# A Conformer convolution whose last channels, layer norm and second product run in two token halves, with weights parted ahead

## The chip, the cores and the metric

The kernel runs on one core of one Trainium2 chip. Its time is device microseconds (us) of one execution. Engines are named as in the profile: PE is TensorE (matmuls; PEld its weight loads), DVE is VectorE, ACT is ScalarE, POOL is GpSimd, SP is SyncE, which here only issues transfers.

## The reference

Two layers over 512 tokens of 1024 channels. Each is a half-step feed-forward, a token mixer and another half-step feed-forward; the mixer of layer 0 is the convolution module that the change is about, that of layer 1 is an attention.

```python
def swiglu_ffn(x, w_gate, w_up, w_down):          # D 1024, F 2816
    return (jax.nn.silu(x @ w_gate) * (x @ w_up)) @ w_down

def conformer_conv(x, w_pw1, b_pw1, w_dw, b_dw, ln_g, ln_b, w_pw2, b_pw2):
    h = x @ w_pw1 + b_pw1                          # 1024 -> 2048
    a, gate = jnp.split(h, 2, axis=-1)
    h = a * jax.nn.sigmoid(gate)
    h = lax.conv_general_dilated(h, w_dw, ...) + b_dw   # causal, 31 taps, each channel by itself
    h = jax.nn.silu(layer_norm(h, ln_g, ln_b))     # mean and variance over the 1024 channels of a token
    return h @ w_pw2 + b_pw2                       # 1024 -> 1024

# layer 0:
h = h + 0.5 * swiglu_ffn(rms_norm(h, ffn1_norm[0]), ...)
h = h + conformer_conv(rms_norm(h, mix_norm[0]), ...)
h = h + 0.5 * swiglu_ffn(rms_norm(h, ffn2_norm[0]), ...)
```

## The kernel before

Activations lie with channels on the 128 partitions and the 512 tokens along the free axis, so a tensor of 1024 channels is eight chunks of 128x512. All is in float32; a product is made of three matmuls on parts: each operand is parted into a rounded high part and the remainder, and `mm3` multiplies high x high, high x low and low x high into one PSUM bank (lines 186 to 188). Weights come from DRAM in units of 128x1024 (512 KB). `fetch` loads a unit on SP's queue into `raw`, ACT casts it to `whi`, and the remainder `wlo` is a subtraction (lines 127 and 128) on DVE, or on POOL for the units 68 to 83 (`POOL_UNITS`), which are the sixteen of the first pointwise product. Three buffers of each are used, and `unit()` takes the oldest pair and starts the next fetch. `weight_order` lists the units in the order of use.

A feed-forward (`ffn`) goes in thirds of its hidden chunks: for each chunk two products `pg` over eight channels of input, Silu and multiplication, parting into `hhi` and `hlo`; then eight products `pd` of the third. The first feed-forward has 44 + 24 units. The convolution stage follows, from the first `pa` product (372.4 us of the profiled execution) to the first `pg` of the next feed-forward (606.6). It does this, per chunk of channels `ch`:

- `gated(ch)`: two products `pa` (48 matmuls), scaled on DVE by the norm's factor `rb`, sigmoid on ACT, the gated product `gl` (with 30 zero columns ahead of the tokens), which is parted into `glh` and `gll` (POOL).
- the 31 taps, each a shifted copy of `gl` times one weight per channel, are dealt out to three engines. `PE_TAPS[ch]` of them are matmuls by diagonal matrices (`taps_pe`, tile `pc`; the diagonals are made on ACT, the first 30 of them during the first feed-forward); `POOL_TAPS[ch]` are scaled on ACT (`pr`) and added on POOL into `accp`, one of the tiles `ws` (line 439); the rest are fused multiply-adds on DVE into `pc` (line 450). Then DVE makes `y` of the parts (line 452).
- statistics: POOL adds `y` into `dsum` and its square into `dsq` (ACT squares).

All of it is at the full 512 tokens. Then comes the layer norm: `token_sums` are matmuls of one column that give the sums over channels, 128 tokens to a column (tiles `ms` and `mq`); DVE takes the variance and its inverse root on tiles of 4 columns (`inv_root`, lines 222 to 230), `spread` brings the mean (`pb_lm`) and the root (`pb_lr`) back to 128x512 with diagonals on ACT and two matmuls, and DVE and POOL subtract the mean. Each chunk is then multiplied by the root, goes through Silu and is parted into `shi` and `slo`. Only then can the second pointwise product start (`second`, tiles `pp`): three outputs together, then five one by one, 192 matmuls of 512 columns. Its results are added to the residual `res`, which lies in the tile `xpar`, and go into the next norm (`n_f2.chunk`).

The order of the instructions on each engine is set by a scheduler when the program is built (it simulates the program as it is written), with a few `tc.issue_after` as bounds. An engine works through its own list strictly in order.

## Time and profile before

| | |
|---|---|
| time, median of three runs | 1993.03 us (1990.7, 1993.03, 1993.52) |
| the profiled execution's own time | 1991.78 us |
| its span in the profile | 1990.1 us |
| mean granted clock of TensorE | 0.981 of full speed |
| busy: PE | 1916.1 us, 96% of the span |
| busy: PEld (weight loads, beside PE) | 1582.6 us, 80% |
| busy: DVE | 1105.6 us, 56% |
| busy: ACT | 751.0 us, 38% |
| busy: POOL | 207.2 us, 10% |
| DRAM traffic | 89 GB/s over the span |

The span is what the profiler recorded of one execution, and the time is somewhat longer than it. Busy time of PE contains overlaps, since matmuls are pipelined: one of 512 columns is shown with 389 ns where the next starts about 0.23 us after it. "Granted clock" is the share of full speed that the chip gave TensorE in a stretch. A row "A <- B" in the table of waits says how long the first engine's instruction waited in sum, and which instruction of which engine released it.

### The profile page before, as it was taken

The page shows a single profiled execution, that of the slowest core. Times are in us where ns is not written, and L with a number is a line of the kernel's source. Part 1 is how long each engine was busy: PE and PEld are TensorE (multiplying, and loading weights), DVE is VectorE, ACT ScalarE, POOL GpSimd, SP SyncE. Part 2 cuts the span into 40 slices and gives each one's busy share as a digit, 9 for nine tenths or more (in the row PEclk, how much of TensorE's full clock was granted, in tenths as well). Part 3 has the DMA queues.
Part 4 walks back from the last instruction along what each step waited for, and adds up shares of the span by engine and source line. Part 5 has one row for each costly group of instructions (what it writes and reads, how often), then busy time and mean ns, then how long its engine had stood idle before and what let it go on. Part 6 is the DMA issues. An engine that isn't in the chain of part 4 may idle for free.

```text
span 1990.1 us, 22242 instructions
## 1 busy us (share of the span) xinstructions
PE 1916.1 (96%) x8705; PEld 1582.6 (80%) x8705; DVE 1105.6 (56%) x1604; ACT 751.0 (38%) x1135; POOL 207.2 (10%) x186
## 2 busy tenths in 40 slices
PE   9999999997579999999999999999999899999997
PEld 6888888886468888888888888887888688888885
DVE  6434434779865434434754444466999754444344
ACT  8323222544553322222432222345777733222222
POOL 0000000374600000000000000002554100000000
PEclk9999999999689999999999999999999999999998
DMA  5333332322013333332333233243223133333321
GB/s 164 98 102 96 96 96 80 111 64 74 1 53 96 96 96 95 97 95 79 112 106 96 95 96 96 90 138 112 72 75 104 48 96 95 96 96 96 98 90 66
DMA packets 54361, 181.98 MB, mean 91 GB/s; under 512 B 6256, under 2 KB 6384, under 8 KB 54256
## 3 DMA queue, kind: packets, MB, share of 16 engines
q1 hardware_dynamic: 53680, 179.52, 29.3%
q8 instruction: 68, 1.11, 0.2%
q10 hardware_dynamic: 576, 1.05, 0.1%
q14 instruction: 37, 0.30, 0.0%
HBM read 172.15 MB, written 4.19 MB: 89 GB/s over the span
## 4 chain that ended last, share of the span: by engine, by line
PE 93%; DVE 5%; ACT 1%; issue 1%; POOL 0%; DMA 0%; SPq 0%; DVEq 0%; ACTq 0%; POOLq 0%
PE pg L186 16%; PE pg L188 16%; PE pg L187 16%; PE pd L187 8%; PE pd L186 8%; PE pd L188 8%; DVE pc L450 3%; PE z L666 2%; PE pa L187 1%; PE pa L188 1%; PE pa L186 1%; PE po L186 1%; PE pv L186 1%; PE pq L186 1%; PE pq L187 1%; PE pv L188 1%
## 5 line engine op out<-in xcount | busy, mean ns | idle before, releaser
L127 ACT CAST whi<-raw 128x1024 fp32r<-128x1024 f32 (+2 forms) x329 | 338.4, 1030 | 1020.3 <-PE pg L187 344.9
L186 PE MATMUL pg<-xhi_f,whi 128*128 128x512 f32 x1408 | 548.3, 390 | 2.8 <-ACT xhi_f L248 1.5
L187 PE MATMUL pg<-xlo_f,whi 128*128 128x512 f32 x1408 | 548.0, 389 | 1.6 <-DVE xlo_f L249 1.6
L188 PE MATMUL pg<-xhi_f,wlo 128*128 128x512 f32 x1408 | 547.7, 389 | 0.1
L128 DVE TENSOR_TENSOR wlo<-raw,whi 128x1024 fp32r<-128x1024 f32 (+2 forms) x313 | 377.5, 1207 | 68.1 <-ACT whi L127 67.7
L186 PEld LDWEIGHTS pg<-xhi_f,whi 128*128 128x128 f32 x1408 | 264.3, 188 | 60.6 <-ACT xhi_f L248 2.8
L187 PEld LDWEIGHTS pg<-xlo_f,whi 128*128 128x128 f32 x1408 | 264.3, 188 | 57.7 <-DVE xlo_f L249 3.0
L188 PEld LDWEIGHTS pg<-xhi_f,wlo 128*128 128x128 f32 x1408 | 264.3, 188 | 55.3 <-DVE wlo L128 0.5
L187 PE MATMUL pd<-hlo,whi 128*128 128x512 f32 x704 | 273.2, 389 | 0.0
L186 PE MATMUL pd<-hhi,whi 128*128 128x512 f32 x704 | 272.6, 389 | 0.0
L188 PE MATMUL pd<-hhi,wlo 128*128 128x512 f32 x704 | 272.6, 389 | 0.0
L304 DVE TENSOR_TENSOR tu<-pg,r_f 128x512 f32<-128x512 f32 x88 | 60.8, 691 | 260.2 <-PE pg L188 259.9
L317 DVE SCALAR_TENSOR_TENSOR xpar<-pd,xpar 128x512 f32<-128x512 f32 x96 | 66.0, 691 | 244.4 <-PE pd L188 244.4
L302 DVE TENSOR_TENSOR tg<-pg,r_f 128x512 f32<-128x512 f32 x88 | 60.8, 691 | 173.7 <-PE pg L188 173.3
L186 PEld LDWEIGHTS pd<-hhi,whi 128*128 128x128 f32 x704 | 132.1, 188 | 27.5
L188 PEld LDWEIGHTS pd<-hhi,wlo 128*128 128x128 f32 x704 | 132.1, 188 | 27.5
L187 PEld LDWEIGHTS pd<-hlo,whi 128*128 128x128 f32 x704 | 132.1, 188 | 27.3
L450 DVE SCALAR_TENSOR_TENSOR pc<-gl,xpar,pc 128x512 f32<-128x512 f32 x141 | 97.5, 746 | 8.6 <-PE pc L188 4.4
L127 ACT CAST hhi<-tu 128x512 fp32r<-128x512 f32 x88 | 55.0, 625 | 68.2 <-DVE tu L305 68.2
L128 POOL TENSOR_TENSOR wlo<-raw,whi 128x1024 fp32r<-128x1024 f32 x16 | 38.7, 2417 | 400.2 <-ACT whi L127 400.2
L565 POOL TENSOR_SCALAR_AFFINE_SELECT tri<-ones 128x128 f32<-128x128 f32 x1 | 0.3, 295 | 734.7 <-DVE tu L305 734.7
L128 DVE TENSOR_TENSOR hlo<-tu,hhi 128x512 fp32r<-128x512 f32 x88 | 60.4, 686 | 8.9 <-ACT hhi L127 8.9
(248 smaller groups left out, 2295.4 us busy)
## 6 DMA issues: line engine op xcount, KB each, us to landing
raw<-in_gu_dram SPq DMA_DIRECT2D x175, 512.0 KB, 3.5
raw<-in_dna_dram SPq DMA_DIRECT2D x64, 512.0 KB, 3.5
raw<-in_dnb_dram SPq DMA_DIRECT2D x32, 384.0 KB, 3.1
raw<-in_pw_dram SPq DMA_DIRECT2D x24, 512.0 KB, 3.5
raw<-in_kq_dram SPq DMA_DIRECT2D x16, 512.0 KB, 3.8
raw<-in_wv_dram SPq DMA_DIRECT2D x8, 512.0 KB, 3.6
raw<-in_wo_dram SPq DMA_DIRECT2D x8, 512.0 KB, 4.2
away<-xpar SPq DMA_DIRECT2D x8, 256.0 KB, 2.1
```

The lines of the kernel that those rows point to most:

```text
L127: ins = A.copy(dst_hi, src)
L128: (G if on_pool else V).tensor_sub(dst_lo, src, dst_hi.bitcast(F32))
L186: PE.matmul(ps, w[0], x[0], start=first, stop=False)
L187: PE.matmul(ps, w[0], x[1], start=False, stop=False)
L188: PE.matmul(ps, w[1], x[0], start=False, stop=last)
L302: V.tensor_mul(tg, pt[0], rb)
L304: V.tensor_mul(tu, pt[1], rb)
L317: V.scalar_tensor_tensor(res[d], pd, 0.5, res[d], op0=ALU.mult, op1=ALU.add)
L450: V.scalar_tensor_tensor(acc, x, q, acc, op0=ALU.mult, op1=ALU.add)
L565: G.affine_select(out=tri, in_=ones, compare_op=ALU.is_ge, fill=0.0, base=0, pattern=[[-1, P]], channel_multiplier=1,)
L666: PE.matmul(dst, st, m[:, a:b], start=False, stop=True, skip_group_check=True)
```

## The change

The change touches the convolution stage, and the first feed-forward ahead of it.

1. **Weights parted ahead.** The 24 units of the two pointwise products are loaded during the first feed-forward, one after each hidden chunk from the third on and two in each row of `pd` products (`part_ahead`). ACT casts them, POOL makes the remainder, and both parts are stored to DRAM (`aparth`, `apartl`), 48 stores issued on ACT's queue. In the convolution `fetch` loads the two parts (2 x 512 KB) straight into `whi` and `wlo`; no cast and no remainder is left there.
2. **Token halves.** Channels 5, 6 and 7 (`HALVED`) go through their taps, statistics and `y` in two halves of 256 tokens. The layer norm and the second product are made once for each half. For the second half the outputs come in the order 5, 6, 7, 0, 1, 2, 3, 4 (`SECOND`); the weights of 5, 6 and 7 are still there, those of the other five are loaded a second time.
3. **Other tables.** `PE_TAPS` and `POOL_TAPS` have new entries, with rows of their own for the second halves; 8 diagonals instead of 30 are made ahead and 30 instead of 6 buffers hold the others; `accp` goes through three tiles instead of two.
4. **A planned order.** `Plan` collects every step of the stage with its engine, an estimated duration, what it reads and writes, a rank and the buffers it takes. `issue` goes through them like a list scheduler (the step that can start first, then by rank) and writes the instructions in that order, under `tc.manual_schedule` for PE, DVE, ACT and POOL.
5. Small: the next feed-forward sums over channels in the order in which they became ready (`norm.order`); the pool `x2` opens after the first feed-forward.

The core of the diff:

```diff
-PE_TAPS = [5, 5, 5, 5, 6, 6, 9, 14]
-POOL_TAPS = [5, 5, 5, 5, 5, 5, 5, 4]
-POOL_UNITS = range(68, 84)
-AHEAD = 30
-E_BUFS = 6
+PE_TAPS = [0, 3, 3, 4, 6, 9, 9, 9]
+POOL_TAPS = [10, 10, 10, 10, 10, 9, 9, 9]
+PE_TAPS_2 = [0, 0, 0, 0, 0, 14, 14, 14]
+POOL_TAPS_2 = [0, 0, 0, 0, 0, 8, 8, 8]
+HALVED = 5
+TOKENS = (slice(0, T // 2), slice(T // 2, T))
+SECOND = (5, 6, 7, 0, 1, 2, 3, 4)
+AHEAD = 8
+E_BUFS = 30
+class Plan:
+    LATE = 0.15
+    SELF = {"V": 0.14, "A": 0.1, "G": 0.02}
+    def add(self, engine, work, do, r=(), w=(), rank=0):
+        ...
+    def issue(self):
+        ...
+                key = (t, steps[n][4])
+                if best is None or key < best[0]:
+                    best = (key, n, new)
...
         yield from feed_forward(0)
-        for c in range(NC):
-            yield pw1[c, 0]
-            yield pw1[c, 1]
-        for d in range(NC):
-            yield pw2[d]
+        for i in range(2 * NC):
+            yield apart[i]
+        for d in (*range(NC), *SECOND[3:]):
+            yield apart[2 * NC + d]
...
+    def part_ahead(p):
+        if behind:
+            i, pair = behind.pop()
+            away = []
+            for n, x in zip("hl", pair):
+                d = spill.tile([P, UNIT], F32, name=f"apart{n}{i}")
+                nc.scalar.dma_start(d, x.bitcast(F32))
+                away.append(d)
+            apart.append(tuple(away))
+        if parting:
+            src, i = parting.pop(0), len(apart)
+            raw = p.tile([P, UNIT], F32, name=f"praw{i}", tag="praw", bufs=2)
+            hi = p.tile([P, UNIT], F32R, name=f"phi{i}", tag="phi", bufs=2)
+            lo = p.tile([P, UNIT], F32R, name=f"plo{i}", tag="plo", bufs=2)
+            nc.sync.dma_start(raw, src)
+            split(hi, lo, raw, on_pool=True)
+            behind.append((i, (hi, lo)))
...
+        if isinstance(src, tuple):
+            pair = []
+            for j, n in enumerate(("whi", "wlo")):
+                t = wp.tile([P, UNIT], F32R, name=f"{n}{i}", tag=n, bufs=3)
+                nc.sync.dma_start(t.bitcast(F32), src[j])
+                pair.append(t)
+            ready.append(tuple(pair))
+            return
...
-            split(hi[:, sl], lo[:, sl], raw[:, sl], on_pool=i in POOL_UNITS)
+            split(hi[:, sl], lo[:, sl], raw[:, sl])
...
+                    if beside is not None and (third or f > 1):
+                        with tc.issue_after(last[0].ins):
+                            beside(pp_)
...
+                    if beside is not None and d in (2, 5):
+                        with tc.issue_after(last[0].ins):
+                            beside(pp_)
...
-    ffn(0, n_f1, n_mix.chunk, early=early_diagonals)
+    parting += [pw1[c, o] for c in range(NC) for o in range(2)] + [pw2[d] for d in range(NC)]
+    ffn(0, n_f1, n_mix.chunk, early=early_diagonals, beside=part_ahead)
...
+        def layer_norm(h, rank):
+            sl, n = TOKENS[h], T // 2
...
+            add("PE", 1.0, lambda: token_sums(ms(), dsum[:, sl], y[NC - 1]()[:, sl]), r=[f"dsum{h}", y7], w=[ms], rank=rank)
...
+                if ch % 2 == 0:
+                    add("V", 0.36, lambda yc=yc: V.tensor_sub(yc(), yc(), lm()), r=[lm], w=[yt], rank=rank)
+                else:
+                    add("G", 0.74, lambda yc=yc: G.tensor_sub(yc(), yc(), lms), r=["lms"], w=[yt], rank=rank)
...
+            gate(ch)
...
+            diagonals(ch, 2 * ch + 1, PE_TAPS[ch])
+            depthwise(ch, TOKENS[0] if ch >= HALVED else ALL, 2 * ch + 3)
+        layer_norm(0, 40)
+        second(0, (0, 1), 50, True)
+        for d in range(2, NC):
+            second(0, (d,), 50 + d, True)
+        for ch in range(HALVED, NC):
+            diagonals(ch, 42, PE_TAPS_2[ch])
+            depthwise(ch, TOKENS[1], 42)
+        layer_norm(1, 45)
+        second(1, SECOND[:2], 90, False)
+        second(1, SECOND[2:3], 91, False)
+        with tc.manual_schedule(engines={nc.tensor.engine, nc.vector.engine, nc.scalar.engine, nc.gpsimd.engine}):
+            plan.issue()
+        for d in SECOND[:3]:
+            n_f2.chunk(d)
+        for d in SECOND[3:]:
+            w = unit()
+            pp = ps.tile([P, T], F32, name=f"pp{d}_1", tag="bank", bufs=8)[:, : T // 2]
...
-        second((0, 1, 2))
-        for d in range(3, NC):
-            second((d,))
```

What stands in a row on an engine shows what the planner made of it. A row is line, operation, result<-operands and the size of the tile; the number behind a name tells its buffer.

On PE, between the last product of the taps and the second pointwise product, before (`pc7` is the last chunk's taps, `ms` and `mq` the sums, `pb_` the spread rows, `pp` the second product):

```order
L426 MATMUL pc7_3806<-y0h_2773,mshift_2726 128x512
L217 MATMUL ms_3937<-onesD_75,dsum_2771 128x1 x4
L217 MATMUL ms_3937<-onesD_75,y7_3930 128x1 x4
L217 MATMUL mq_3964<-onesD_75,dsq_2772 128x1 x4
L217 MATMUL mq_3964<-onesD_75,sqy7_3933 128x1 x4
L207 MATMUL pb_lm_3950<-dg_lm_0_3951,onesr_73 128x512
L207 MATMUL pb_lm_3950<-dg_lm_1_3957,onesr_73 128x512
L207 MATMUL pb_lr_3991<-dg_lr_0_3992,onesr_73 128x512
L207 MATMUL pb_lr_3991<-dg_lr_1_3998,onesr_73 128x512
L186 MATMUL pp0_4078<-shi0_4014,whi84_3554 128x512
L186 MATMUL pp1_4079<-shi0_4014,whi85_3699 128x512
```

And in the changed kernel (`pc7_256` is the second token half of the last chunk, `pb_lm0` and `pb_lr0` belong to the first half's layer norm, `pp0_0` is output 0 of the first half):

```order
L325 MATMUL pc7_256_4257<-glh7_4024,d229_4220 128x256
L326 MATMUL pc7_256_4257<-gll7_4039,d229_4220 128x256
L327 MATMUL pc7_256_4257<-glh7_4024,d229_4220 128x256
L728 MATMUL pb_lm0_4372<-dg_lm0_0_4339,onesr_73 128x256
L325 MATMUL pc7_256_4257<-glh7_4024,d230_4239 128x256
L326 MATMUL pc7_256_4257<-gll7_4039,d230_4239 128x256
L327 MATMUL pc7_256_4257<-glh7_4024,d230_4239 128x256
L728 MATMUL pb_lm0_4372<-dg_lm0_1_4359,onesr_73 128x256
L669 MATMUL pc7_256_4257<-y0h_2886,mshift_2876 128x256
L728 MATMUL pb_lr0_4406<-dg_lr0_0_4396,onesr_73 128x256
L728 MATMUL pb_lr0_4406<-dg_lr0_1_4399,onesr_73 128x256
L325 MATMUL pp0_0_4436<-shi0_4419,whi84_3767 128x256
```

Nothing stood between the sums and `pp0` but the spread rows; now the taps of the other half stand among them, to the end of `pc7_256`.

On DVE, the layer norm's small steps, before:

```order
L450 SCALAR_TENSOR_TENSOR acc7_3916<-gl7_3763,xpar_70,acc7_3916 128x512
L454 TENSOR_TENSOR y7_3930<-acc7_3916,y7_3930 128x512
L488 COPY sm_3936<-ms_3937 128x4
L196 CAST dp_lm_3947<-sm_3936 128x4
L494 TENSOR_TENSOR sm_3936<-sm_3936 128x4
L197 TENSOR_TENSOR dp_lm_3947<-sm_3936,dp_lm_3947 128x4
L495 TENSOR_TENSOR sm_3936<-mq_3964,sm_3936 128x4
L496 TENSOR_SCALAR sm_3936<-sm_3936 128x4
L223 TENSOR_SCALAR sm_3936<-sm_3936 128x4
L224 TENSOR_SCALAR sm_3936<-sm_3936 128x4
```

And now, in the first half's layer norm (`sm0` has two columns for each quantity):

```order
L690 SCALAR_TENSOR_TENSOR pc6_256_4166<-gl6_3758,xpar_70,pc6_256_4166 128x256 x3
L713 COPY sm0_2889<-ms0_4309 128x2
L690 SCALAR_TENSOR_TENSOR pc6_256_4166<-gl6_3758,xpar_70,pc6_256_4166 128x256
L719 CAST dp_lm0_2890<-sm0_2889 128x2
L720 TENSOR_TENSOR dp_lm0_2890<-sm0_2889,dp_lm0_2890 128x2
L690 SCALAR_TENSOR_TENSOR pc6_256_4166<-gl6_3758,xpar_70,pc6_256_4166 128x256
L737 TENSOR_TENSOR sm0_2889<-sm0_2889 128x2
L738 TENSOR_TENSOR sm0_2889<-mq0_4322,sm0_2889 128x2
L739 TENSOR_SCALAR sm0_2889<-sm0_2889 128x2
L363 TENSOR_SCALAR sm0_2889<-sm0_2889 128x2
L364 TENSOR_SCALAR sm0_2889<-sm0_2889 128x2
```

Taps of the second half of chunk 6 (`pc6_256`) have come between the small steps.

On POOL around the end of the taps, before (`ws3` collects the last chunk's scaled taps, line 504 subtracts the mean, which lies in `ws4`):

```order
L439 TENSOR_TENSOR ws3_2769<-ws3_2769,pr232_3907 128x512
L439 TENSOR_TENSOR ws3_2769<-ws3_2769,pr233_3910 128x512
L439 TENSOR_TENSOR ws3_2769<-ws3_2769,pr234_3913 128x512
L468 TENSOR_TENSOR dsum_2771<-dsum_2771,y6_3800 128x512
L469 TENSOR_TENSOR dsq_2772<-dsq_2772,sqy6_3802 128x512
L504 TENSOR_TENSOR y5_3627<-y5_3627,ws4_2770 128x512
L504 TENSOR_TENSOR y6_3800<-y6_3800,ws4_2770 128x512
L504 TENSOR_TENSOR y7_3930<-y7_3930,ws4_2770 128x512
```

And at this place now, behind the first half's last addition of chunk 7:

```order
L679 TENSOR_TENSOR ws2_2881<-ws2_2881,pr201_256_4315 128x256
L679 TENSOR_TENSOR ws4_2883<-ws4_2883,pr176_256_4301 128x256
L679 TENSOR_TENSOR ws2_2881<-ws2_2881,pr202_256_4320 128x256
L679 TENSOR_TENSOR ws2_2881<-ws2_2881,pr203_256_4330 128x256
L679 TENSOR_TENSOR ws2_2881<-ws2_2881,pr204_256_4370 128x256
L679 TENSOR_TENSOR ws2_2881<-ws2_2881,pr205_256_4377 128x256
L748 TENSOR_TENSOR y1_3504<-y1_3504,lms0_2891 128x256
L748 TENSOR_TENSOR y3_3797<-y3_3797,lms0_2891 128x256
L748 TENSOR_TENSOR y5_3989<-y5_3989,lms0_2891 128x256
L748 TENSOR_TENSOR y7_4299<-y7_4299,lms0_2891 128x256
```

The scaled taps of the second half (`pr201` to `pr205` here) stand ahead of the four subtractions of the mean `lms0`.

On ACT, in the first feed-forward at the end of the first third, before (`tg` is the Silu of the last hidden chunk, `whi` a weight cast, `hhi` the cast of the hidden chunk):

```order
L303 ACTIVATE tg0_7_845<-tg0_7_845 128x512
L127 CAST whi18_815<-raw18_814 128x1024
L127 CAST hhi0_7_851<-tu0_7_846 128x512
L127 CAST whi19_856<-raw19_855 128x1024
L127 CAST whi20_888<-raw20_887 128x1024
```

And now (`phi` is the cast of a weight that is parted ahead, `aparth` and `apartl` are stores):

```order
L447 ACTIVATE tg0_7_863<-tg0_7_863 128x512
L279 DMA aparth4_873<-phi4_796 128x1024
L279 DMA apartl4_875<-plo4_797 128x1024
L234 CAST phi5_878<-praw5_877 128x1024
L279 DMA aparth5_979<-phi5_878 128x1024
L234 CAST phi6_984<-praw6_983 128x1024
L279 DMA aparth6_1085<-phi6_984 128x1024
L234 CAST whi18_833<-raw18_832 128x1024
L279 DMA apartl5_981<-plo5_879 128x1024
L234 CAST hhi0_7_869<-tu0_7_864 128x512
L279 DMA apartl6_1087<-plo6_985 128x1024
L234 CAST phi7_1090<-praw7_1089 128x1024
L234 CAST whi19_884<-raw19_883 128x1024
```

Three weights are parted between that Silu and the casts that followed it.

## Rows read from the trace of the kernel before

**Rows 1.** Page, part 2: PE busy, in tenths, in 40 slices.

```profile
PE   9999999997579999999999999999999899999997
```

**Rows 2.** Windows: start:end, busy us of PE, PEld, DVE, ACT, POOL, PEclk, DMA share, GB/s.

```profile
30.00:372.40 342.40, 342.40 (x1512) 283.44 (x1511) 160.92 (x205) 108.19 (x150) 4.87 (x3) 1.00 0.31 97
372.40:606.60 234.20, 188.62 (x796) 152.61 (x795) 179.45 (x286) 110.22 (x192) 103.91 (x75) 0.88 0.18 57
372.40:480.40 108.00, 108.00 (x478) 88.78 (x476) 83.18 (x132) 42.94 (x58) 57.49 (x38) 1.00 0.26 81
480.40:561.00 80.60, 35.13 (x131) 26.98 (x130) 70.53 (x122) 46.77 (x104) 46.41 (x37) 0.67 0.03 11
```

**Rows 3.** Tiles pc and pp: count: min/mean/max ns, first to last, shape.

```profile
L187 PE MATMUL pc<-gll,dh x55: 388/396/628, 399.7 to 514.2; 128*128 128x512 f32 x55
...
L187 PE MATMUL pp<-slo,whi x64: 388/389/797, 560.9 to 606.2; 128*128 128x512 f32 x64
```

**Rows 4.** Waits, 480 to 562 us: sum us, count, longest.

```profile
PE ms L217 <- POOL dsum L468: 23.3, 1, 23.3
```

**Rows 5.** Chain of waits, 480 to 606 us: start, us, engine, tile, count.

```profile
484.57 11.20 DVE pc L450 x17
```

**Rows 6.** Timeline of PE (start, us); weight loads of tile pv.

```profile
1327.86 0.28 PE L188 MATMUL pv<-whi,kvl 128*128 128x256 f32 x1
1327.98 0.28 PE L186 MATMUL pv<-whi,kvh 128*128 128x256 f32 x1
...
L186 PEld LDWEIGHTS pv<-whi,kvh x128: 187/188/201, 1327.4 to 1513.8; 128*128 128x128 f32 x128
```

**Rows 7.** Groups by shape, DVE: count, busy us, mean ns, idle before.

```profile
L677 DVE SCALAR_TENSOR_TENSOR a<-z,a 128x512 f32<-128x512 f32 x32 | 21.9, 683 | 4.0 <-ACT a L676 3.9
...
L677 DVE SCALAR_TENSOR_TENSOR a<-z,a 128x384 f32<-128x384 f32 x16 | 8.8, 551 | 0.6 <-ACT a L676 0.6
```

**Rows 8.** Groups by shape, POOL; line 697 alone.

```profile
L439 POOL TENSOR_TENSOR ws<-ws,pr 128x512 f32<-128x512 f32 x31 | 39.7, 1284 | 1.4 <-ACT pr L438 0.4
...
L128 POOL TENSOR_TENSOR gll<-gl,glh 128x542 fp32r<-128x542 f32 x8 | 10.9, 1360 | 2.7 <-ACT glh L127 2.7
...
L697 POOL TENSOR_TENSOR a<-a x12: 733/792/1714, 1375.5 to 1524.1; 128x256 f32<-128x256 f32 x12
```

**Rows 9.** Timeline of PE, 543 to 561 us; in brackets the wait.

```profile
543.48 1.85 PE L217 MATMUL mq<-onesD,sqy 128*128 128x1 f32 x8
...
560.94 0.80 PE L187 MATMUL pp<-slo,whi 128*128 128x512 f32 x1 [1.08 <-DVE slo L128]
```

**Rows 10.** Timeline of POOL and DVE, 379 to 383 us.

```profile
379.69 2.41 POOL L128 TENSOR_TENSOR wlo<-raw,whi 128x1024 fp32r<-128x1024 f32 x1 [3.68 <-ACT whi L127]
...
379.96 2.16 DVE L223 TENSOR_SCALAR rs_mix<-v_mix 128x4 int32<-128x4 int32 x1
...
382.15 0.17 DVE L224 TENSOR_SCALAR rs_mix<-rs_mix 128x4 int32<-128x4 int32 x1
```

**Rows 11.** Windows, PE alone: busy us, PEclk, DMA share, GB/s.

```profile
490.00:495.00 5.00, 0.00 (x0) 0.52 0.00 0
...
500.00:505.00 5.00, 5.00 (x22) 0.96 0.01 3
```

**Rows 12.** DMA issues (KB, us to landing); issues on ACT; GB/s in 0 to 30 us.

```profile
raw<-in_pw_dram SPq DMA_DIRECT2D x24, 512.0 KB, 3.5
...
L770 ACTq DMA_DIRECT2D out_dram<-out x4: 338/356/374, 1982.3 to 1984.9; - x4
...
GB/s 0 0 80 324 306 219 259 330 339 333 360 393 431 415 401 410 423 415 300 87 11 0 0 0 0 87 251 360 93 218 328 87 131 322 229 22 0 0 0 76
```

**Rows 13.** Timeline of ACT, 80 to 104 us.

```profile
95.00 1.06 ACT L127 CAST whi<-raw 128x1024 fp32r<-128x1024 f32 x1 [3.11 <-PE pg L187]
...
95.96 0.63 ACT L303 ACTIVATE tg<-tg 128x512 f32<-128x512 f32 x1
```

**Rows 14.** Tile hhi, 20 to 130 us.

```profile
L186 PE MATMUL pd<-hhi,whi x44: 389/389/389, 100.4 to 129.7; 128*128 128x512 f32 x44
```

More of the change, by code (lines that the diff above doesn't have):

```diff
@@ L159, in decoder_kernel @@
     count = [0]
+    apart = []
+    parting, behind = [], []
+    def part_ahead(p):
[15 more added lines that the diff above has]
+            behind.append((i, (hi, lo)))
     def fetch(parts=1, then=None):
@@ new lines, in pe3, with do @@
+        def pe3(ps_, w, x, first, last, sl, r, rank=0, pre=None):
+            def do():
+                if pre is not None:
+                    pre()
+                mm3(ps_(), w(), x(), first, last)
+            add("PE", 0.68 * size(sl) + 0.02 * (sl != ALL), do, r=r, w=[ps_], rank=rank)
+        ssm, pbm = bank("ss_mix", 4), bank("pb_mix")
+        small = tp.tile([P, 4], F32, name="rs_mix_0", tag="rs", bufs=1)
+        vmix = tp.tile([P, 4], F32, name="v_mix_0", tag="v", bufs=1)
+        dgm = []
@@ new lines, in mix_diagonals @@
+        def mix_diagonals():
+            V.tensor_scalar_add(vmix, ssm(), RMS_EPS)
+            inv_root(small, vmix, "mix_0")
+            parts = tp.tile([P, 8], F32R, name="dp_mix_0", tag="dp", bufs=1)
+            V.tensor_copy(parts[:, :4], small)
+            V.tensor_sub(parts[:, 4:], small, parts[:, :4].bitcast(F32))
+            for h in range(2):
+                dgm.append(tp.tile([P, T], F32R, name=f"dg_mix_0_{h}", tag="sq", bufs=2))
+                for b in range(4):
+                    one = parts[:, 4 * h + b : 4 * h + b + 1].bitcast(F32)
+                    V.tensor_scalar_mul(dgm[h][:, b * P : (b + 1) * P], ident, one)
@@ new lines, in decoder_kernel, with gate @@
+        add("-", 5.0, lambda: None, w=["acc"])
+        add("PE", 0.7, lambda: token_sums(ssm(), *n_mix.parts), r=["acc"], w=[ssm], rank=-2)
+        add("V", 8.0, mix_diagonals, r=[ssm], w=["dgm"], rank=-2)
+        for h in range(2):
+            add("PE", 0.23, lambda h=h: PE.matmul(pbm(), onesr, dgm[h], start=h == 0, stop=h == 1), r=["dgm"], w=[pbm], rank=-2)
+        add("A", 0.6, lambda: A.copy(rb, pbm()), r=[pbm], w=["rb"], rank=-2)
+        gated, weights = {}, {}
+        def gate(ch):
@@ new lines, in gate, with diagonals, do @@
+            gated[ch] = gl, glh, gll
+        def diagonals(ch, rank, n):
+            for t in range(n):
+                if (ch, t) in diags:
+                    continue
+                q = ch * KW + t
+                d = Buf("e", lambda q=q: cv.tile([P, 2, P], F32R, name=f"d{q}", tag="e", bufs=E_BUFS))
+                def do(d=d, q=q):
+                    A.activation(d()[:, 0], ident, AF.Copy, scale=wdh[:, q : q + 1].bitcast(F32))
+                    A.activation(d()[:, 1], ident, AF.Copy, scale=wdl[:, q : q + 1])
+                add("A", 0.54, do, w=[d], rank=rank)
+                diags[ch, t] = d
@@ new lines, in depthwise @@
+        def depthwise(ch, sl, rank):
+            gl, glh, gll = gated[ch]
+            h, f = sl.start, size(sl)
+            half = f < 1
+            n_pe, n_pool = (PE_TAPS_2 if h else PE_TAPS)[ch], (POOL_TAPS_2 if h else POOL_TAPS)[ch]
+            pc = bank(f"pc{ch}_{h}", sl.stop - sl.start)
+            at0 = slice(0, sl.stop - sl.start)
+            for t in range(n_pe):
+                d = diags[ch, t]
+                pe3(pc, lambda d=d: pair(d),
+                    lambda t=t: [g()[:, t + h : t + sl.stop] for g in (glh, gll)],
+                    t == 0, ch < 2 and t == n_pe - 1, sl, [glh, gll] + ([d] if isinstance(d, Buf) else []), rank=rank)
+            if n_pe and ch > 1:
+                add("PE", 0.23 * f, lambda: PE.matmul(pc(), mshift, y0h[:, sl], start=False, stop=True),
+                    r=["y0h"], w=[pc], rank=rank)
+            accp, at_ = ws[2 + ch % 3][:, sl], ("accp", ch % 3, h)
@@ new lines, in second, with pre @@
+        def second(h, ds, rank, take):
+            sl = TOKENS[h]
+            pp = [bank(f"pp{d}_{h}", T // 2) for d in ds]
+            for k in range(NC):
+                for j, d in enumerate(ds):
+                    def pre(d=d):
+                        if take:
+                            weights["2", d] = unit()
+                    pe3(pp[j], lambda d=d, k=k: at(weights["2", d], k * P, P), lambda k=k: [x()[:, sl] for x in s[k]],
+                        k == 0, k == NC - 1, sl, [("shi", k, h), ("slo", k, h), s[k][0], s[k][1]], pre=None if k else pre, rank=rank)
+            for j, d in enumerate(ds):
+                add("V", 0.4, lambda j=j, d=d: V.scalar_tensor_tensor(
+                    res[d][:, sl], pp[j](), col("b_pw2", d), res[d][:, sl], op0=ALU.add, op1=ALU.add),
+                    r=[pp[j]], w=[("res", d)], rank=rank)
```

360 lines of the change are left out of this document (232 added, 128 removed).

## The prediction, made before the changed kernel ran

> **What bounds the kernel now.** I read the page first, by slices: PE is at nine tenths in almost every slice and dips in two places, slices 10 to 14 and near 31 [rows 1]. The change touches the first dip. A table by stage sizes it [rows 2]: the feed-forward ahead of it (30 to 372.4 us) has PE busy all 342.4 us, so nothing is to be won there. The convolution runs from the first `pa` product at 372.4 to the first `pg` of the next feed-forward at 606.6, 234.2 us. In its first 108.0 us PE does 478 products without a gap, 0.226 us each. In the next 80.6 us PE is busy 35.1 at a mean clock of 0.67, while DVE is busy 70.5.
>
> The products themselves: 384 `pa`, 165 taps in `pc`, 192 `pp` (a third of the last two stands in [rows 3]) and 8 mean shifts, 749 x 0.226 = 169 us. So 65 of the 234 us are waiting and slow clock. The waits of the second stretch name the place [rows 4]: the longest, 23.3 us, is PE's for POOL's `dsum` at the channel sums. The chain there is mostly DVE taps, 17 in 11.20 us, 0.66 each [rows 5]. Every channel must be through its 31 taps, and then through the layer norm, before the second product can start, and by then PE has nothing else.
>
> **The change, part by part.** The order of the changed program shows that PE gets half-token taps and half of the second product to do while DVE, ACT and POOL finish the other half. My sum follows PE's queue through the stage, counting from its first `pa` product, which stays where it is: the 1608 PE rows ahead of it are the same but for the first norm's sums and spread, which move a few rows.
>
> *PE's work* hardly changes. 384 `pa` and 52 full-width products (48 taps, 4 shifts) at 0.226 make 98.5 us. 213 half-width tap products and 384 half-width `pp` go at 0.12, the pace of the 256-column products in `pv`, which start at 1327.86 and 1327.98 [rows 6]: 71.6 us. With the small sums, some 174 us.
>
> [...]
>
> *A, to the end of the first half's sums.* Three queues have to arrive. PE has 98.5 us, 197 half taps at 0.12 (23.6) and 1.5 of sums: 124. DVE starts once the norm's factor is out, which stands behind 63 products and two sums on PE, about 16.5 us in. It then has 89 full taps, 24 gate steps and 7 additions at 0.66 (79.2), and 52 half taps and 3 half additions. For a half tap no row exists; a step with the same operation takes 683 ns at 512 columns and 551 at 384 [rows 7], 1.03 ns a column, so 0.66 less 0.26 is 0.39. That is 21.5 us, and DVE is through at 117. POOL starts near 21 us (factor, gate, first scaled tap) and has 45 full additions and 8 of statistics at 1.30, 7 remainders at 1.36, and 28 half additions at 0.75 (shortest 256-column one 733 ns) [rows 8]: 99.6 us, to 121. Behind POOL stand `y7`, its square and the sums, 2.5 us. Three queues that end within 7 us of each other and feed each other lose something: I take 128, bounds 124 (PE alone) and 140. DVE's saving is real: 154 taps x 0.66 were 102 us, now 89 x 0.66 + 66 x 0.39 = 84, and 8 weight remainders leave it.
>
> *B, the first layer norm.* Before, from the last `mq` sums (543.48 + 1.85) to the first `slo` product at 560.94 are 15.6 us [rows 9], at full width. Halving takes some 6.5 off (half the diagonals, one subtraction instead of five between root and spread, shorter steps ahead of the first `slo`): 9. But a cost comes in which the trace shows only once or twice. At 379.69 POOL runs a subtraction of 2.41 us; DVE's `rs_mix` step on four columns, both sides in SBUF, starts at 379.96 and lasts 2.16, the next one 0.17 [rows 10]. DVE was held until POOL was through. Before, POOL is mostly idle in the variance chain. In the changed order POOL has 12 half additions for the other tokens and 4 subtractions queued exactly there, and DVE has 15 such small steps and then two more. With six of POOL's sixteen done by then, ten are left: at 0.73 each, 7.3 us if every one holds one step, none if they fall between. I take 5, so B is 14, bounds 9 and 21.
>
> [...]
>
> *C, half of the second product beside the rest of the taps*, to the second half's sums: 105 half products, 12.6 us on PE. DVE has 16 scalings and remainders, 10 half taps, 3 additions and 4 results, 12.5 us at 0.36 to 0.39; POOL 13 half additions, 9.8. Two things come on top. PE has just been idle for long: after the idle stretch before 496 us its clock stood at 0.52, and it was back at 0.96 only over 500 to 505 [rows 11]; some four microseconds at half rate cost 2. And the fourth weight pair is fetched when the first is done: two loads of 512 KB, 3.5 us each from issue to landing, together about 5.2 since the engines move up to 431 GB/s [rows 12], against 2.6 of cover. I take 16, bounds 13 and 20.
>
> *D, the second layer norm*: 87 half products (10.4 us) cover a chain of about 12 (the 9 of B with sums ahead and two or three held steps): 12, bounds 10.4 and 16.
>
> *E, the rest of the second product.* Two outputs together (5.8), a third (2.9), then five whose weights are fetched again. The first refetch waits for a buffer that the pair frees: 5.2 us against 3.2 of cover, 2.0 of stall. After that 1 MB per 2.9 us is needed, 362 GB/s, under the peak of rows 12, so 14.4: 25 us, bounds 23 and 30. The next feed-forward's first three raw weights stand ahead of all this in SP's queue, and its products begin with the channels that are ready first, so nothing is added behind.
>
> A to E: 128 + 14 + 16 + 12 + 25 = **195 us** in place of 234.2, **39 us** off.
>
> *The parting of the weights* moves into the first feed-forward: 24 casts and 48 stores on ACT, 24 remainders on POOL, 24 loads on SP. POOL is idle there. ACT is busy 108 of 342 us [rows 2]; 24 casts of 1.06 [rows 13] and 48 issues of 0.36 [rows 12] add 43. Queued behind them are the `hhi` casts and the weight casts that PE needs. The tightest place is the end of a third, where three parts stand behind one Silu. Before, that Silu starts at 95.96 [rows 13], and the `pd` products at 100.4 [rows 14]; in PE's order 29 of them come before the first that reads the last `hhi`, so it is due near 107. In the new order four store issues, two casts, the landing of a store (3.5 us as a load's) and a weight cast stand between: from 96.6 that is about 104, so it is 2 to 3 us in time. I cost it at nothing; if that cover were gone, three such places would cost a few us each, and bound the cost at 10. SP's new loads wait only for a POOL step long done.
>
> The profiled execution took 1991.78 us, its span 1990.1; the median of the runs is 1993.03, 1.25 above. 1991.78 - 39 = 1952.8, and beside the median **1954 us**.
>
> **The rivals.** *Clean run*: nothing is held and the queues meet as planned: 124 + 9 + 13 + 10.4 + 23.5 = 180, so 54 off, 1939. For it: PE ran 108 us without a gap before. Against: rows 10, and three full queues. *Drift*: queues in a fixed order get out of step, A 136, B 19, C 19, D 15, E 28 = 217: 17 off, 1976. For it: DVE, POOL and PE all over nine tenths in A, so each late step is passed on. *No gain*: drift of 35 us or more in A alone leaves the time within 0.2%. *Slower*: weight loads in the first feed-forward come late. Its DMA traffic rises from 97 GB/s [rows 2] by 38 MB in about 300 us to some 220. Each of the 68 weights has three raw buffers' lead: its load starts when the remainder of the third weight ahead is done, and its cast must wait until that weight's products end, some 14 us later. It lands in 3.5 [rows 12]; from a landing of about 14 us on, it is the load that is late. 1 us at each of 68 would take back the 39 and 29 more: 2022. Against: the peak of rows 12 is nearly twice that. [...]
>
> **How the numbers follow.** Forecast (about 1943 to 1967) 0.58, clean 0.12, drift 0.19, no gain 0.04, slower 0.07 with the rule on loads in it. The predicted time is the forecast's. The range, 1938 to 1976, spans from the clean run to drift; what lies above holds about 0.15. About 0.2%, 4 us, is what a measurement of this kernel tells from no change: faster 0.89, same 0.04, slower 0.07.
>
> **What would show it.** Right: the first `pg` of the next feed-forward near 567 us; DVE's small steps of the first layer norm mostly at 0.7 instead of 0.16 us, and few held in the second; PE idle 10 to 18 us ahead of the first `pp`, at a low clock; a gap of 2 us ahead of the fourth output of the second half; PE without a gap from 30 to 372. Wrong: gaps of PE among the `pa` products (A is mis-sized), `hhi` late at the end of a third, or half products further apart than 0.12 us at full clock.

## The result

The changed kernel takes 1981.19 us (median of four runs, 1980.09 to 1984.59) beside 1992.57 before: 0.9947 of the time, 95% interval 0.993 to 0.9964. It is faster, by 11.4 us where 39 were forecast, and outside the range of 1938 to 1976. The profiled execution of the changed kernel is the longest of its four, 1984.59 us, so the spans of the two profiled executions are 7.3 us apart where the medians are 11.4 apart.

Cut at the first `pa`, the first `pg` behind the convolution, the first `pv` and the last `po` product, the two profiled executions (and those of two experiments told below) divide like this, in us:

| stretch | before | after | difference | e1_back | e8_four |
|---|---|---|---|---|---|
| start and first feed-forward | 372.4 | 376.0 | +3.6 | 371.9 | 371.9 |
| convolution | 234.2 | 199.8 | -34.4 | 198.5 | 188.0 |
| second and third feed-forward | 721.0 | 735.0 | +14.0 | 721.1 | 721.1 |
| attention and its output product | 283.5 | 289.5 | +6.0 | 286.7 | 283.6 |
| last feed-forward and end | 379.0 | 382.6 | +3.6 | 379.0 | 379.0 |
| span | 1990.1 | 1982.8 | -7.3 | 1957.2 | 1943.6 |

The stage that was changed gained 34.4 us. Four stages that were not meant to change lost 27 between them.

Inside the convolution, the windows of the changed kernel by the parts A to E of the prediction (columns as in [rows 2]; after the start and end: us, then busy us of PE, PEld, DVE, ACT, POOL, then PEclk, DMA share, GB/s):

```profile
375.96:503.31 127.35, 126.42 (x661) 108.39 (x660) 111.01 (x204) 97.37 (x213) 101.83 (x99) 1.00 0.38 141
503.31:517.48 14.17, 3.96 (x22) 2.97 (x22) 13.57 (x34) 7.92 (x21) 8.97 (x13) 0.73 0.00 1
517.48:537.21 19.73, 17.81 (x122) 17.20 (x122) 11.57 (x30) 8.78 (x22) 7.37 (x10) 0.85 0.50 190
537.21:549.54 12.33, 12.33 (x93) 12.33 (x92) 10.11 (x35) 7.49 (x21) 2.83 (x4) 0.86 0.34 125
549.54:575.77 26.23, 23.71 (x195) 23.13 (x193) 16.71 (x29) 13.59 (x23) 0.00 (x0) 1.00 0.64 227
```

In the first row PE is busy 126.42 of 127.35 us: the gap that [rows 2] show in the second half of the taps is gone. The 23.3 us of [rows 4] are gone too; the longest waits of PE from there to the end of the stage are these (us in total, times, longest):

```profile
PE pb_lr L728 <- ACT dg_lr L726: 7.6, 1, 7.6
PE pp L327 <- DMA wlo<-apartl: 2.0, 3, 0.9
PE pp L325 <- ACT shi L759: 1.9, 1, 1.9
PE pp L325 <- DMA whi<-aparth: 1.3, 2, 0.7
```

Where the loss comes from stands in the products of a feed-forward. The tile `pd` in the changed kernel (count: shortest, median, longest in ns, first and last start), and two rows of PE's timeline in a stretch without a gap:

```profile
L325 PE MATMUL pd<-hhi,whi x704: 392/392/398, 100.4 to 1965.0; 128*128 128x512 f32 x176
...
L326 PE MATMUL pd<-hlo,whi x704: 387/398/398, 100.7 to 1965.2; 128*128 128x512 f32 x176
...
699.66 0.39 PE L325 MATMUL pd<-hhi,whi 128*128 128x512 f32 x1
...
705.95 0.40 PE L325 MATMUL pd<-hhi,whi 128*128 128x512 f32 x1
```

Before, the same product lasted 389 ns in every record [rows 14]. From the first row of the timeline to the second are 27 products, 6.29 us: 0.233 us each. In the trace before, 18 of these products stand in 4.08 us, 0.2267 each:

```profile
729.80 0.39 PE L186 MATMUL pd<-hhi,whi 128*128 128x512 f32 x1
...
733.88 0.39 PE L186 MATMUL pd<-hhi,whi 128*128 128x512 f32 x1
```

The granted clock is 1.00 in both kernels there, and no engine is waited for. By the starts of the products in the two traces, the 2112 of `pd` stand 6.6 ns further apart on average, which is 13.9 us, and so do the 1056 `pg` of the second feed-forward, 7.0 us. The other 6.0 of the 27 are in the attention, where not all of it comes from the pace (below).

What differs is where the operands lie. Before, the weights (`whi`) begin 64 bytes past a multiple of 256 in each partition, and so does nearly everything that is streamed against them. The layer norm of the changed kernel has four new tiles of four columns (`dp_lm0`, `dp_lr0`, `dp_lm1`, `dp_lr1`), for which the pool `tp` lays out 32 bytes each. All that is allocated behind `tp` now starts 128 bytes further on, modulo 256; the pools there also come in another order. From the two built programs (start in bytes of the lowest tile, remainder by 256):

```
tile                              before          after
whi (weights)                     48192    64     48192    64
xhi of the first feed-forward     72768    64     72768    64
last tile of the pool tp         114208    32    114336   160
hhi of the first feed-forward    187968    64    132800   192
xhi of the second feed-forward   130624    64    140992   192
kvh (attention)                  114240    64    114368   192
```

The products that slowed are those whose streamed operand moved: `pd`, the second feed-forward's `pg`, and `pk` and `po` in the attention. The `pg` of the first, third and last feed-forward and the `pa`, whose operands stayed, did not.

### The profile page after: what moved, and what is told of

It reads as the page before. It is cut to its first block, busy times and chain, and to the rows that moved or that the text cites. A ratio compares the mean times of both kernels' runs of the same rounds, so it can differ in the third digit from the quotient of the medians.

```text
span 1982.8 us, 23270 instructions
## 1 busy us (share of the span) xinstructions
PE 1938.9 (98%) x8991; PEld 1594.9 (80%) x8993; DVE 1089.9 (55%) x1646; ACT 787.8 (40%) x1222; POOL 278.4 (14%) x261
## 3 DMA queue, kind: packets, MB, share of 16 engines
q1 hardware_dynamic: 62032, 209.93, 33.1%
## 4 chain that ended last, share of the span: by engine, by line
PE 88%; DVE 5%; ACT 3%; issue 1%; POOL 1%; DMA 1%; SPq 0%; DVEq 0%; POOLq 0%; ACTq 0%
PE pg L327 16%; PE pg L325 16%; PE pg L326 16%; PE pd L327 8%; PE pd L326 8%; PE pd L325 8%; PE z L946 1%; DVE pc L690 1%; PE pa L326 1%; PE pa L327 1%; PE pa L325 1%; PE po L325 1%; PE po L326 1%; PE po L327 1%; POOL ws L679 1%
## 5 line engine op out<-in xcount | busy, mean ns | idle before, releaser
L234 ACT CAST whi<-raw 128x1024 fp32r<-128x1024 f32 (+2 forms) x305 | 313.0, 1028 | 940.8 <-PE pg L326 376.9
L235 DVE TENSOR_TENSOR wlo<-raw,whi 128x1024 fp32r<-128x1024 f32 (+2 forms) x305 | 368.6, 1210 | 63.9 <-ACT whi L234 63.6
L326 PE MATMUL pd<-hlo,whi 128*128 128x512 f32 x704 | 277.4, 395 | 0.0
L327 PE MATMUL pd<-hhi,wlo 128*128 128x512 f32 x704 | 276.8, 395 | 0.0
L325 PE MATMUL pd<-hhi,whi 128*128 128x512 f32 x704 | 276.7, 395 | 0.0
L235 POOL TENSOR_TENSOR plo<-praw,phi 128x1024 fp32r<-128x1024 f32 x24 | 57.5, 2400 | 283.4 <-ACT phi L234 281.8
L679 POOL TENSOR_TENSOR ws<-ws,pr 128x256 f32<-128x256 f32 (+1 forms) x90 | 90.8, 1019 | 28.3 <-ACT pr L677 24.6
L690 DVE SCALAR_TENSOR_TENSOR pc<-gl,xpar,pc 128x512 f32<-128x512 f32 (+1 forms) x154 | 91.9, 639 | 2.8 <-PE pc L669 1.1
```

Of the source, the lines that this page charges most:

```text
L234: ins = A.copy(dst_hi, src)
L235: (G if on_pool else V).tensor_sub(dst_lo, src, dst_hi.bitcast(F32))
L325: PE.matmul(ps, w[0], x[0], start=first, stop=False)
L326: PE.matmul(ps, w[0], x[1], start=False, stop=False)
L327: PE.matmul(ps, w[1], x[0], start=False, stop=last)
L679: add("G", 1.28 * f + 0.1 * half, lambda pr=pr: G.tensor_add(accp, accp, pr()[:, at0]), r=[pr], w=[at_], rank=rank)
```

## The experiments on the address

The theory to test was that the place of the streamed operand sets the pace. The rival was that busier engines, or the parting's traffic, slow TensorE. **e1_back** moves the changed kernel's tiles back with a padding that the kernel has anyway:

```diff
-LEAN_TP, LEAN_DG = 384, 64
+LEAN_TP, LEAN_DG = 256, 64
```

> The changed kernel with one padding tile ahead of the small tiles cut from 384 to 256 bytes, so that every tile behind it lies 128 bytes lower, at 64 past a multiple of 256 as in the kernel before, instead of 192. Nothing else differs. Theory (the start address of the streamed operand sets the pace of a product): the pd products of all four feed-forwards go back from 233 to 226.6 ns apart, the pg products of the second feed-forward too; the first pa product comes back from 376.0 to about 372.4 us, and from the first pg of the second feed-forward to the end it takes 1383.5 us instead of 1407.0. Time 1981.2 less 22 to 27, so 1954 to 1959 us. Rival (the chip gives TensorE less because the engines are busier, or the parting's traffic slows it): the pd products stay at 233 ns and the time at 1977 to 1985 us.

Measured: 1959.47 us (1957.61 to 1960.52), 0.9835 of before (0.982 to 0.985), 21.7 us less than the changed kernel and half a microsecond above what was expected. The pace is back:

```profile
L325 PE MATMUL pd<-hhi,whi x704: 389/389/389, 99.9 to 1939.4; 128*128 128x512 f32 x176
```

The three feed-forward stretches in the table above are those of before. Only the attention keeps 3.2 us of its loss. **e2_before_shifted** does the opposite to the kernel before, with nothing of the change in it:

```diff
-LEAN_TP, LEAN_DG = 384, 64
+LEAN_TP, LEAN_DG = 512, 64
```

> The kernel before with that padding tile raised from 384 to 512 bytes, so that everything behind it lies 128 bytes higher, at 192 past a multiple of 256. Nothing of the change is in it. Theory of the address: the pd products go from 226.6 to about 233 ns apart and those pg products that stream from behind the padding too; the time rises from 1992.6 by 22 to 27 us to 2015 to 2020 us. Rival (busier engines, or the parting): 1989 to 1997 us.

Measured: 2011.96 us (2011.03 to 2012.45), 1.0099 of before (1.0084 to 1.0114), 20.2 us lost, somewhat less than was expected. In its `pd`:

```profile
L186 PE MATMUL pd<-hhi,whi x704: 390/393/404, 99.8 to 1992.6; 128*128 128x512 f32 x176
```

So 128 bytes of padding, without any of the change's work, bring the slow pace. The rival falls. **e3_table** asks which addresses are slow. It computes nothing of the model: series of 48 products in the kernel's pattern, `mov` with the streamed operand and `wei` with the weights at a chosen offset, the other at 64. It was executed once.

```diff
+MOVES = [("a", 0), ("b", 32), ("c", 64), ("d", 96), ("e", 128), ("f", 160), ("g", 192), ("h", 224),
+         ("i", 320), ("j", 448), ("k", 4), ("l", 68), ("m", 196)]
+LOADS = [("n", 0), ("o", 64), ("p", 128), ("q", 192), ("r", 32)]
...
+    def series(name, m, w, n=T):
+        m, w = m // 4, w // 4
...
+                a = slice(w + k * P, w + (k + 1) * P)
+                b = slice(m + k * T, m + k * T + n)
...
+                PE.matmul(pp[:, :n], wh[:, a], mh[:, b], start=first, stop=False)
+                PE.matmul(pp[:, :n], wh[:, a], ml[:, b], start=False, stop=False)
+                PE.matmul(pp[:, :n], wl[:, a], mh[:, b], start=False, stop=last)
```

> Nothing of the model is computed: series of 48 products, three by three as in the kernel, each with the streamed operand (mov) at a given number of bytes past a multiple of 512 and the weights at 64, then series with the streamed operand at 64 and the weights (wei) elsewhere, and half-width series. Theory of the address: movg (192) 233 ns apart, movc (64) 226.6, movj (448) as movg and movi (320) as movc; 0, 32, 96, 128, 160 and 224 are not known beforehand; the weights' own place changes nothing. If it is the distance between the two operands that counts, weiq (weights at 192, stream at 64) is as slow as movg. Rival (the address does nothing): all at 226 to 228 ns.

One of the three rows of eight series; the first and last start are 45 products apart:

```profile
L110 PE MATMUL movc<-mh,wh x16: 389/389/395, 51.6 to 61.8; 128*128 128x512 f32 x16
...
L110 PE MATMUL mova<-mh,wh x16: 394/394/394, 29.2 to 39.7; 128*128 128x512 f32 x16
...
L110 PE MATMUL move<-mh,wh x16: 388/388/398, 73.7 to 84.0; 128*128 128x512 f32 x16
...
L110 PE MATMUL movg<-mh,wh x16: 392/395/398, 95.9 to 106.4; 128*128 128x512 f32 x16
...
L110 PE MATMUL weio<-mh,wh x16: 389/389/389, 185.7 to 195.9; 128*128 128x512 f32 x16
...
L110 PE MATMUL wein<-mh,wh x16: 393/394/394, 174.7 to 185.0; 128*128 128x512 f32 x16
...
L110 PE MATMUL weip<-mh,wh x16: 393/396/398, 196.6 to 207.1; 128*128 128x512 f32 x16
...
L110 PE MATMUL weiq<-mh,wh x16: 390/393/404, 207.8 to 218.3; 128*128 128x512 f32 x16
```

In order: stream 64 (`movc`), 0, 128, 192, then weights 64 (`weio`), 0, 128, 192. Some 10.2 us are 227 ns a product, 10.3 are 229 and 10.5 are 233. The last three rows have the stream at 64, the place that was thought to be the good one, and two of them are slow. Sorted by stream less weights, modulo 256, the series agree (by the unrounded starts): distance 0 (`movc`, `weio`, `movi` at 320, and `movc` run again at the end) 226.9 to 227.7 ns, 64 (`move`, `wein`) 229, 128 (`movg`, `weiq`, `movj` at 448) 232.5 to 233.4, 192 (`mova`, `weip`) 233.3 to 233.4. That 320 is as fast as 64 and 128 bytes off is slow is what makes it 256. The theory as it was first put, by the stream's own address, falls; the distance takes its place. Two runs ask for it in the whole kernel. **e5_before_all** moves weights and streams of the kernel before together:

```diff
     spill = ctx.enter_context(tc.tile_pool(name="spill", bufs=1, space=bass.MemoryType.DRAM))
+    lean(const, 128)
```

> The kernel before with 128 bytes of padding ahead of the weight buffers, so that the weights, the streamed operands and all else behind move up together: weights and streams both at 192 past a multiple of 256. After the table of start addresses the theory is that the distance between streamed operand and weights counts (0 modulo 256 is fast), not the address: pd and pg stay at 226.6 ns, the time at 1990 to 1994 us. Rival (the stream's own address counts, 192 is slow): all pg, pd, pa, pp at 233 ns and 2035 us or more.

Measured: 1992.73 us, 1.0002 of before (0.9993 to 1.0012). Weights and streams are both at 192, and nothing slowed. **e6_before_weights** moves the weights alone:

```diff
-LEAN_TP, LEAN_DG = 384, 64
+LEAN_TP, LEAN_DG = 128, 64
...
+    lean(wp, 128)
+    lean(xp, 128)
```

> The kernel before with the weight buffers alone moved up by 128 bytes (weights at 192, all streamed operands where they were modulo 256, at 64; paddings of 128 bytes ahead of the weights and behind them, and the one of 384 bytes cut to 128). Theory of the distance: every product of a weight unit slows from 226.6 to 232 to 233 ns; some 7490 products of 512 columns x 6 ns are 45 us, so 2032 to 2040 us. Rival (the stream's address counts): unchanged, 1990 to 1994 us.

Measured: 2032.3 us (2030.44 to 2034.14), 1.0204 of before (1.0189 to 1.0219), 40.6 us lost, with the products 232.4 ns apart. Some 7490 of them at 5.6 ns more are 42 us, and the spans of the two profiled executions are 42.3 apart. The distance it is. Why the chip behaves so no run shows.

## The experiments on the convolution

The first layer norm's cost by steps that POOL holds was a term of the forecast (B). DVE's timeline in the changed kernel (start, us):

```profile
507.87 0.65 DVE L370 SCALAR_TENSOR_TENSOR sm<-rt_ln,sm 128x2 f32<-128x2 f32 x1
508.56 0.65 DVE L368 TENSOR_TENSOR rt_ln<-sm 128x2 f32<-128x2 f32 x1
509.24 0.65 DVE L369 SCALAR_TENSOR_TENSOR rt_ln<-sm,rt_ln 128x2 f32<-128x2 f32 x1
...
505.44 0.16 DVE L738 TENSOR_TENSOR sm<-mq,sm 128x2 f32<-128x2 f32 x1
...
538.84 0.16 DVE L369 SCALAR_TENSOR_TENSOR rt_ln<-sm,rt_ln 128x2 f32<-128x2 f32 x1
```

POOL works without a gap there, and a step on two columns takes 0.65 us, seven times in a row from 507.87 on. The one that reads `mq` from PSUM takes 0.16 (fourth row). That row alone shows little, since two steps near it with both sides in SBUF are as short (at 506.19 and 507.07). In the second half's layer norm (last row) every step up to the root takes 0.16 while POOL rests; the two behind the root stand beside POOL's subtractions and take 0.47 and 0.66. **e4_back_psum** starts from e1_back and gives every small step one operand in PSUM:

```diff
-            ms, mq = bank(f"ms{h}", 2), bank(f"mq{h}", 2)
+            ms, mq = bank(f"ms{h}", 2), bank(f"mq{h}", 16)
+            raw_mean, varp, root = lambda: ms(), lambda: mq()[:, 2:4], lambda: mq()[:, 4:6]
...
+                V.tensor_copy(var, varp())
+                y, v, t = root(), var, tmp
...
+                    V.tensor_mul(t, y, v)
+                    V.scalar_tensor_tensor(t, t, -0.5, y, op0=ALU.mult, op1=ALU.mult)
+                    V.scalar_tensor_tensor(y, t, 1.5, y, op0=ALU.add, op1=ALU.mult)
```

> The shifted-back changed kernel, with the layer norm's small steps on DVE rewritten so that each reads one operand from PSUM (the root and the variance lie in the bank of the sums; one small copy more for each half). Theory of the held steps (DVE steps with SBUF on both sides wait for POOL's instruction to end): the small steps of the first half's layer norm last 0.15 to 0.25 us instead of 0.65, the stretch from the end of its sums to its first product on slo goes from 14.3 us to 9 to 10, and the time is 3 to 5 us under that of the shifted-back kernel alone. Rival (they are long because they follow each other closely, or the gain is given back by the second half's taps, which are due later): within 1 us of it.

Measured: 1955.27 us (1951.61 to 1957.3), 0.9818 of before (0.9802 to 0.9835), 4.2 under e1_back. DVE and POOL at the same place:

```profile
502.36 0.16 DVE L749 SCALAR_TENSOR_TENSOR sm<-sm,mq 128x2 f32<-128x2 f32 x1
502.55 0.17 DVE L750 SCALAR_TENSOR_TENSOR mq<-sm,mq 128x2 f32<-128x2 f32 x1
...
497.56 6.04 POOL L679 TENSOR_TENSOR ws<-ws,pr 128x256 f32<-128x256 f32 x8
```

POOL is as busy as it was in B (8.97 us, 8.96 in e1_back), and all the steps take 0.15 to 0.17: B fell from 14.1 us in e1_back to 9.5, as the theory has it. Beside a POOL at work, the steps with both sides in SBUF mostly took 0.65 us in the changed kernel and in e1_back, and those with one operand in PSUM 0.15 to 0.17 here. Why a step beside POOL lasts longer no run shows.

**e8_four** adds to this a fourth pair of weight buffers for the second product, to test what the loads cost there:

```diff
+                tag = "raw" if i - 68 in (19, 23, 27) else n
-                t = wp.tile([P, UNIT], F32R, name=f"{n}{i}", tag=n, bufs=3)
+                t = wp.tile([P, UNIT], F32R, name=f"{n}{i}", tag=tag, bufs=3)
...
                             weights["2", d] = unit()
+                            if d == 0:
+                                fetch()
...
-            w = unit()
+            w = ready.pop(0) if d == SECOND[-1] else unit()
```

> The kernel with the layer norm's small steps in PSUM, and a fourth pair of weight buffers for the second product: every fourth pair goes into two of the three raw buffers, which lie idle there, and one load more is ahead. Theory (the last waits for loads, 2.6 us in sum ahead of the fourth and fifth output of the first half and the first refetched ones of the second, are due to three pairs of buffers): these waits go, the second product ends 2 to 3.5 us earlier, 1952 to 1953.5 us beside 1955.3. Rival (other waits take their place, or raw buffers held longer delay the next feed-forward): within 1 us of 1955.3, or above it.

Measured: 1945.76 us (1944.93 to 1948.26), 0.9772 of before (0.9757 to 0.9786), the fastest of all; more was gained than was expected. Its windows C, D and E:

```profile
508.90:525.20 16.30, 16.28 (x121) 16.28 (x122) 11.32 (x30) 8.31 (x21) 7.41 (x10) 0.87 0.44 160
525.20:536.00 10.80, 10.80 (x92) 10.80 (x92) 9.28 (x35) 6.99 (x19) 2.82 (x4) 1.00 0.62 248
536.00:559.90 23.90, 23.24 (x194) 23.05 (x193) 15.52 (x27) 12.62 (x22) 0.00 (x0) 1.00 0.59 222
```

PE has no idle time left in C, and C and E are 2.9 and 2.1 us shorter than in e4_back_psum: the waits for loads are gone, PE's idle time in the two parts fell by 3.1 us, and the mean clock in C is 0.87 instead of 0.83. The two profiled spans are 6.3 us apart, 5.0 of them in the convolution and 1.3 in the attention. The medians are 9.5 apart because the profiled execution of e4_back_psum is its fastest, 3.7 under its median; where its others lose that, no trace shows. The program's scheduler, which orders the attention, can order it otherwise after an edit in another stage. In the changed kernel, e1_back and e4_back_psum PE's rows there stand in one and the same order, which is not that of before; in e8_four they stand as before, row for row. The stretch in the profiled executions:

```profile
1291.50:1578.20 286.70, 277.92 (x1504) 232.32 (x1505) 233.37 (x399) 186.74 (x345) 93.24 (x92) 0.99 0.29 84
...
1280.90:1564.60 283.70, 274.28 (x1507) 232.40 (x1506) 235.41 (x399) 186.27 (x345) 90.73 (x92) 0.99 0.29 85
```

The first is e1_back, the second e8_four; before took 283.5, and e4_back_psum 284.9 in the order of e1_back. So the other order goes with 1.3 to 3.2 us in these traces. The order by itself was not tried, and 1 to 2 us of this stretch also come and go with short stretches of low clock (at 0.50 for 3.4 us twice in the trace before, for 6.8 and 3.4 in that of the changed kernel): e4_back_psum has half as much of it there as e1_back and e8_four.

**e7_not_ahead** undoes the parting ahead, in e1_back:

```diff
-        for i in range(2 * NC):
-            yield apart[i]
+        for c in range(NC):
+            yield pw1[c, 0]
+            yield pw1[c, 1]
         for d in (*range(NC), *SECOND[3:]):
-            yield apart[2 * NC + d]
+            yield pw2[d]
...
-            split(hi[:, sl], lo[:, sl], raw[:, sl])
+            split(hi[:, sl], lo[:, sl], raw[:, sl], on_pool=i in range(68, 84))
```

> The shifted-back changed kernel with the parting of the weights undone: the 24 units and the five that are needed twice are loaded raw in the convolution and parted there, ACT casts, POOL makes the remainders of the first sixteen and DVE the others, as before; a unit's fetch stands behind the last product of the unit that frees its buffer. The planned order is made without knowing of these steps. Theory (POOL is nearly full up to the first half's sums, so 16 remainders of 2.42 us, 39 us, push that end out): the stretch from the first pa to the first half's sums goes from 127 us to 150 to 166, and the time to 1985 to 2000 us. Rival (the halves alone bring the gain and the remainders find room): 1958 to 1966 us.

Measured: 2005.52 us (2003.41 to 2005.9), 1.0067 of before (1.0052 to 1.0082), slower than before and than was expected. A in this run, two of its longest waits, and the remainders:

```profile
371.90:540.80 168.90, 139.13 (x661) 116.25 (x660) 118.12 (x208) 115.20 (x237) 138.55 (x114) 0.90 0.18 57
...
ACT pr L679 <- POOL ws L681: 44.0, 30, 4.4
...
POOL wlo L235 <- ACT whi L234: 22.6, 13, 5.6
...
L235 POOL TENSOR_TENSOR wlo<-raw,whi x16: 2348/2397/2467, 364.8 to 489.6; 128x1024 fp32r<-128x1024 f32 x16
```

A grew from 127.3 us in e1_back to 168.9. POOL works 36.8 us more (138.55 for 101.77), and it also waits for casts that stand in ACT's planned queue behind other work. With these tables and this order, the halves depend on a POOL that the parting has emptied. The order was planned without the casts and remainders; how much of the loss comes from that, and how much the halves alone could bring with tables and an order of their own, was not tried.

## Why the prediction was wrong

The direction held, and so did the mechanism in the stage: four of its five parts came within 1.2 us. In us, forecast and measured:

| part | forecast | changed kernel | e8_four |
|---|---|---|---|
| A, to the first half's sums | 128 | 127.3 | 127.4 |
| B, the first layer norm | 14 | 14.2 | 9.6 |
| C, to the second half's sums | 16 | 19.7 | 16.3 |
| D, the second layer norm | 12 | 12.3 | 10.8 |
| E, the rest | 25 | 26.2 | 23.9 |
| sum | 195 | 199.8 | 188.0 |

- **The step that failed** is the one from the stage to the kernel: the sum took 39 us off the whole execution, with all that lies outside the convolution left as it was, and the first `pa` product "stays where it is". It came 3.6 us later, and 23.6 more were lost behind the stage. The working rested on PE's order, in which the rows ahead and behind are nearly the same. The same products in the same order took 3% longer (233.3 ns apart for 226.7) where their operands had moved. The rivals were all mechanisms inside the stage or the parting; none had a change of layout.
- A sign of it was in the rows that were read. The taps stream from places that move by 4 bytes a tap, and the mean in `pc` was 396 ns where `pp` had 389 [rows 3]. It was taken as one pace, 0.226; in the trace before, the `pc` products up to 480 us stand 233 ns apart.
- **A** came out by a different split. PE is idle 0.9 us in it, so the 4 us that were allowed for three queues out of step were mostly PE's own work, 126.4 us where 124 were summed.
- **C** was too small by 3.7 us. Its own working had 12.6 for the products, 2 for the clock and 2.6 for loads without cover, which with 1.8 for the sums are 19; 16 was taken. e8_four, in which the loads are covered, has 16.3.
- **B** was right, size and cause, and e4_back_psum shows the cause: without held steps B is 9.5 us, where the working had 9 and 5 for holding. The held steps came as forecast, mostly 0.65 us in the first layer norm and two held in the second. **D** came out at 12.3 with a mean clock of 0.86, which was not in its sum; in e1_back, at 1.00, it took 11.1.
- **Half products** at 0.12 us: right. In the changed kernel the half taps of A stand 119 ns apart, and in e3_table the half-width series go at 117.8 to 119.8 ns at all four offsets that were tried. The loads of 187 to 192 ns beside them are not added to that. The chance of "slower" has a rule on loads in it; no run shows such a rule, and these products show none of its cost.
- **The parting** was costed at nothing, and that held. PE has no gap from 30 to 372.4 us, the first `pd` starts at 100.4 as before, and the cast of the last `hhi` of the first third starts at 103.32, where 104 was worked out:

```profile
30.00:372.40 342.40, 342.40 (x1497) 280.70 (x1496) 159.10 (x189) 122.49 (x144) 57.55 (x24) 1.00 0.61 204
...
103.32 0.62 ACT L234 CAST hhi<-tu 128x512 fp32r<-128x512 f32 x1 [1.85 <-DVE tu L449]
```

  The count of products is the only sign of the loss in the first row: 1497 in 342.4 us, where there were 1512 [rows 2]. "PE without a gap" was named as the test of this stretch, and a PE that is busy throughout and slower passes it.

With the layout put back (e1_back), the time is 1959.47 us, inside the forecast's own range of 1943 to 1967 and 5.5 over the number: the stage took 198.5 us for 195, and the attention, in its other order, 3.2 more than before.

## What to carry to other kernels

Before a change is costed, compare the start addresses of the operands of the busiest engine in both programs: a few small tiles in an early pool move everything behind them, and here 128 bytes took 21.7 of 33.1 us. Where an engine is busy all the time, compare the spacing of its instructions instead of looking for gaps. Small steps on DVE that stood beside a busy POOL were freed here by keeping one of their operands in PSUM (0.65 us each without it, 0.15 to 0.17 with it), and transfers that waited for buffers by lending them buffers that lay idle in that stage (PE's 3.3 us of waits for loads in the changed kernel were gone in e8_four).
